# A hybrid Fourier, recurrence and expert layer on one core: A gate tiles between the recurrence heads, adaLN blocks spread, expert buffers at multiples of 512 bytes

## The chip, the cores and the metric

The kernel runs on one core of a Trainium2 chip. The metric is device microseconds of one execution, the median of several runs. The core has a matrix engine (TensorE, PE in the profile; PEld is its weight load), a vector engine (VectorE, DVE), an activation engine (ScalarE, ACT), GpSimd (POOL) and SyncE (SP), which here only issues transfers.

## The reference, cut to what matters

One layer of a diffusion backbone: 512 latent tokens and 256 context tokens of 1024 elements.

```python
z    = modulate(rmsnorm(x, norm1_g), sh1, sc1) @ w_in   # columns: Fourier 512 | X 1024 | G 1024 | A 1024 | B 1024
u    = dwconv(z[X], conv_w, conv_b)                     # width 4, context and latent tokens
r, i = sigmoid(u @ wa + ba), sigmoid(u @ wi + bi)       # 8 heads of 128, two directions
a    = exp(-8 * r * softplus(-lam))
h    = scan over tokens: h = a * h + sqrt(1 - a * a) * i * u    # forward + backward, context first
y    = sigmoid(z[A]) * (fourier(z[F]) @ w_four) + sigmoid(z[B]) * ((gelu(z[G]) * h) @ w_lru)
x    = x + g1 * (y @ w_out)
h2   = modulate(rmsnorm(x, norm2_g), sh2, sc2)
s    = softmax(h2 @ w_router)                           # 16 experts take their 64 best tokens
x    = x + g2 * scatter(s * (silu(xg @ w_gate) * (xg @ w_up)) @ w_down)   # 1024 -> 1536 -> 1024
out  = rmsnorm(x, final_g)
```

`sh1`, `sc1`, `g1` and so on are the six adaLN sections of 1024 columns of `silu(c) @ w_ada + b_ada`.

## The kernel before, in words

Everything before the experts is float32 work on TensorE as three products of split operands: a float32 weight `raw` is split into `wH` (a cast to fp32r, L229) and `wL = raw - wH` (a DVE subtraction, L230), and `mm3` (L426) multiplies H·H, H·L and L·H. Weights come in tiles of 1024 rows × 256 columns (1 MB), listed in `W` (L150 to L173) and loaded by SP in the order of `seq` into three `raw` buffers (`load_next`, L177); `split(j)` consumes tile j, in two halves of 128 × 1024 elements each, and `use(j)` splits the next tile while it hands over this one.

The order of the work is the order of the program: each engine takes its instructions as they are written (`manual_schedule`), and semaphores do the rest. PSUM has two tags of two slots of 2 banks each, `z` (`zt`) and `g` (`gt`); `ct` takes one or the other in turn.

*Recurrence heads.* Eight heads h; for each, 8 k-steps of 6 matmuls (512 latent and 256 context columns, tile `zX` in `z`). In k-steps 4 to 7 of head h, one gate (two matmuls, L674, L675, tile `ga` in `g`, tanh on ACT at L677) of head h−1 follows each step. After the matmuls `conv(h)` (L663, L667) runs on DVE; then `lru(h-1)`: tanh on ACT and `stt` on DVE (L688), exp and sqrt on ACT, `stt` on DVE (L698), a multiplication on GpSimd (L699), twice for two directions, then three scans on DVE (L705, L707, L709) and an addition on GpSimd (L711). At even heads the next X weight is split in the middle of `lru`, its cast on DVE.

*A, G and B tiles.* Eight A tiles follow (24 matmuls of 512 columns, `zcols`), with `a_evac` (tanh on ACT, L750, and a DVE multiplication into `y4`, L751), the last head's gates and `lru`; then eight G tiles (gelu times the recurrence, split into `gH`, `gL`); then eight B tiles, each with a `w_lru` tile; then the output projection `zO` and the routing.

*adaLN.* The first eight blocks of 256 columns are computed before the heads. The other sixteen are done by `ada_acc` (L264: on DVE, eight scaled additions of 128 × 256 elements and a sum, L271 to L276) and `ada_red` (L280: a matmul with ones, L287 or L291, and additions on DVE), one behind each pair of A, G, B or `w_lru` tiles and the last in `zO`.

*Experts.* From 475 us on, 16 experts: gate, up (L1116), `silu`, down (L1210, L1267), scatter (L1132). Their weights, 128 rows × 6144 bytes a load (768 KB), come by SP through a ring of 22 buffers: unit n goes to slot n modulo 22 (`eload`, L834 to L861). Slots 0 to 13 are the pool `ra` on the right side of SBUF, 14 to 18 the pool `rb` and 19 the pool `rc` on the left, 20 and 21 two `held` tiles on the left (`wd`, `we`). A buffer is loaded anew when its user is done.

Of the kernel before, what the change touches and what calls it, by code (L numbers as in the profile page):

```python
# [9 lines left out]
F32 = mybir.dt.float32  # L10
# [7 lines left out]
P = 128  # L18
D = 1024
# [57 lines left out]
def layer(ctx: ExitStack, tc: tile.TileContext, I, out):  # L77
# [48 lines left out]
    eps_t = keep.tile([P, 1], F32, name="eps_t")  # L126
    ones = keep.tile([P, 1], F32, name="ones")
# [4 lines left out]
    cs = keep.tile([P, KD, 32], F32, name="cs")  # L132
# [20 lines left out]
    W += [(cols(w_in, D_F + 256 * i), 8) for i in range(4)]  # L153
    W += [(cols(w_in, D_F + 2 * D + 256 * i), 8) for i in range(4)]
# [5 lines left out]
    J_X, J_A, J_G, J_B, J_O = 2, 6, 10, 14, 22  # L160
# [4 lines left out]
    ada_at = {j: [p] for j, p in zip([J_A] + list(range(J_A + 2, J_O)), range(8, 23))}  # L165
    ada_at[J_O + 1] = [23]
# [97 lines left out]
    def ada_acc(i):  # L264
        for j in ada_at.get(i, ()):
            raw = take("a", j)
            r = [stage.tile([P, 256], F32, tag="acc", bufs=2, name=f"acc{j}_{a}") for a in range(2)]
            m = len(r)
            for k in range(KD):
                if k < m:  # L270
                    dve.tensor_scalar(r[k], raw[:, k, :], cs[:, k, 0:1], None, op0=OP.mult)  # L271
                else:
                    dve.scalar_tensor_tensor(r[k % m], raw[:, k, :], cs[:, k, 0:1], r[k % m], op0=OP.mult, op1=OP.add)
            load_next()
            if m == 2:
                dve.tensor_add(r[1], r[0], r[1])  # L276
            adaq.append((j, r[-1]))
# [32 lines left out]
    zs = st_p.tile([P, NT, 1028], F32, name="zs")  # L310
    rs, ce = zs[:, 0, 0:1024], zs[:, 1, 0:512]
# [368 lines left out]
    def lru(h, mid=None, pre=None):  # L680
        u = U.pop(h)
        r = {(d, i): GP.pop((h, d, i)) for d in range(2) for i in range(2)}
        tps = {}
        for d in range(2):
            q = 8 * d + h
            tps[d] = lr.tile([P, TA], F32, tag="tp", bufs=3, name=f"tp{h}")
            act.activation(tps[d], r[d, 0], AF.Tanh, bias=c2[:, q:q + 1], scale=c2[:, q:q + 1])
            dve.scalar_tensor_tensor(r[d, 1], r[d, 1], 1.0, u, op0=OP.add, op1=OP.mult)  # L688
        if pre:
            pre()  # L690
        for d in range(2):
            q = 8 * d + h
            act.activation(r[d, 0], r[d, 0], AF.Exp, bias=c4n[:, q:q + 1], scale=c4n[:, q:q + 1])
        for d in range(2):
            act.activation(tps[d], tps[d], AF.Sqrt, scale=0.25)
        for d in range(2):
            a, b, s = r[d, 0], r[d, 1], tps[d]
            dve.scalar_tensor_tensor(s, a, 1.0, s, op0=OP.add, op1=OP.mult)  # L698
            pool.tensor_tensor(b, s, b, op=OP.mult)  # L699
        if mid:  # L700
            mid()
        for d in range(2):
            a, b, s = r[d, 0], r[d, 1], tps[d]
            if d == 0:
                dve.tensor_tensor_scan(s, a, b, 0.0, OP.mult, OP.add)  # L705
            else:
                dve.tensor_tensor_scan(s[:, 0:TC][:, ::-1], a[:, 0:TC][:, ::-1], b[:, 0:TC][:, ::-1],  # L707
                                       0.0, OP.mult, OP.add)
                dve.tensor_tensor_scan(s[:, TC:TA][:, ::-1], a[:, TC:TA][:, ::-1], b[:, TC:TA][:, ::-1],  # L709
                                       s[:, 0:1], OP.mult, OP.add)  # L710
        pool.tensor_tensor(yr[:, h, :], tps[0][:, TC:TA], tps[1][:, TC:TA], op=OP.add)  # L711

    GATES = [(0, 0), (0, 1), (1, 0), (1, 1)]
    AT = {4: 0, 5: 1, 6: 2, 7: 3}
    load_gw(0)
    for h in range(H):
        if h % 2 == 0:
            w = SP.pop(J_X + h // 2)
        zf = f2(zt(f"zX{h}"))
        for k in range(KD):  # L720
            wH, wL = ch(w, k, h % 2)
            n = 0
            for a, b, bc in ((wH, hH, cH), (wH, hL, cL), (wL, hH, cH)):
                f, l = k == 0 and n == 0, k == KD - 1 and n == 2
                pe.matmul(zf[:, 512:1024], a, b[:, k, :], start=f, stop=l)
                pe.matmul(zf[:, 256:512], a, bc[:, k, :], start=f, stop=l)
                n += 1
            if h and k in AT:
                gate(h - 1, *GATES[AT[k]])
        if h + 1 < H:  # L730
            load_gw(h + 1)
        conv(h, zf[:, 256:1024])

        def next_split(h=h):
            if h % 2 == 0:
                split(J_X + h // 2 + 1, dve.tensor_copy)
        if h:
            lru(h - 1, next_split)
        else:
            next_split()  # L740


# [10 lines left out]
    def last_gates(k):  # L753
        if k % 2:
            gate(H - 1, *GATES[k // 2])
        if k == 1:
            a_evac(0, zz_[0])
        if k == 4:
            split(J_A + 1)

    for i in range(4):
        w = SP.pop(J_A + i) if i < 2 else use(J_A + i)
        zz_ = []
        for c in range(2):
            z = ct(c if i else 0, "zA")
            zz_.append(z)
            zcols(w, z, c, None if i or c == 0 else last_gates)
        evacs = lambda: [a_evac(2 * i + c, zz_[c]) for c in range(0 if i else 1, 2)]
        if i == 1:
            lru(H - 1, pre=lambda: split(J_A + 2, dve.tensor_copy), mid=evacs)  # L770
            close_lr()
            close_hc()
        else:
            evacs()
        ada_red()
        ada_acc(J_A + i)

    gp, close_gp = sb("gp", "right")
    gH = gp.tile([P, H, T], F32R, name="gH")
    gL = gp.tile([P, H, T], F32R, name="gL")  # L780
    for i in range(4):
        w = use(J_G + i)
        for c in range(2):
            z = ct(c, "zG")
            zcols(w, z, c)
            j = 2 * i + c
            act.activation(z, z, AF.Gelu_apprx_tanh)
            dve.tensor_mul(yr[:, j, :], z, yr[:, j, :])
            act.copy(gH[:, j, :], yr[:, j, :])
            dve.tensor_sub(gL[:, j, :], yr[:, j, :], gH[:, j, :].bitcast(F32))  # L790
        ada_red()
        ada_acc(J_G + i)

# [3 lines left out]
    for i in range(4):  # L797
        w = use(J_B + 2 * i)
        th = sg.tile([P, 2, 512], F32, tag="th", bufs=2, name="thB")
        for c in range(2):  # L800
            z = ct(c, "zB")
            zcols(w, z, c)
            act.activation(th[:, c, :], z, AF.Tanh, scale=0.5)
        ada_red()
# [19 lines left out]
    rings = [None] * 3  # L824
    rings[0], close_ra = sb("ra", "right")
# [124 lines left out]
    ada_red()  # L950
# [354 lines left out]
    close_ra()  # L1305
    close_stage()
# [32 lines left out]
```

## Time and the profile before

| | |
|---|---|
| Runs, median (lowest to highest of 3) | 1206.58 us (1205.19 to 1206.61) |
| The profiled execution: time, span | 1205.73 us, 1203.9 us |
| Mean granted clock of TensorE | 0.984 |
| Busy: PE, PEld, DVE, ACT, POOL | 95%, 57%, 47%, 24%, 9% |
| Moved by DMA, mean | 368.01 MB, 306 GB/s |

The span is the profiled execution from its first to its last instruction; what the device counts around it makes up the rest of its time. Busy shares are means over stages with different limits, so they are read by stage. In the page's strip of 40 slices (30.1 us each) the heads, A and G tiles lie in slices 4 to 11, the experts from slice 16 on. A timeline's row gives start, duration, engine, line, operation, output and inputs, and in brackets the idle time before it and what ended it; "issue" is a wait that no event of the profile explains.

### The profile page before, as it was taken

Reading aid. Unit: us, or ns where it says so; the run is one execution under the profiler, and the core shown is the slowest. Engines: PE = TensorE matmul, PEld = TensorE weight load, DVE = VectorE, ACT = ScalarE, POOL = GpSimd, SP = SyncE. Lnnn points to the kernel's source line nnn. Section 1 sums busy time; section 2 is a strip of 40 time slices with the busy share of each in tenths; the row PEclk is TensorE's granted clock in tenths of the full one; section 3 lists DMA queues with packets and bytes.
Section 4 is the critical chain, followed back from the end, with each engine's and each line's share of the span. In section 5 each row is a group of like instructions: output and inputs, shape, how many; then the busy total and the mean of one; then the engine's idle time right before and its main releaser. Section 6 shows DMA issues by size and latency. Waiting matters only on the chain. (4 is left out here: it accounts for less than half of the span.)

```text
span 1203.9 us, 16716 instructions
## 1 busy us (share of the span) xinstructions
PE 1148.4 (95%) x6891; PEld 684.3 (57%) x6891; DVE 564.3 (47%) x1053; ACT 286.4 (24%) x448; POOL 112.9 (9%) x118
## 2 busy tenths in 40 slices
PE   8979988899999999999999999999999999999986
PEld 5768766588888897545445445445345345345333
DVE  5566899996776675233332332332232232232024
ACT  5443766644322223101001001001001001001004
POOL 5164443310000000000000000000000000000002
PEclk9989988999999999999999999999999999999998
DMA  8922011155555495899899999999999999999995
GB/s 308 300 89 88 18 53 53 35 173 177 188 180 191 149 390 206 313 379 418 356 422 419 418 420 421 418 419 421 420 417 421 421 418 418 422 421 418 419 400 211
DMA packets 115435, 368.01 MB, mean 306 GB/s; under 512 B 8912, under 2 KB 61656, under 8 KB 115232
## 3 DMA queue, kind: packets, MB, share of 16 engines
q1 hardware_dynamic: 112688, 363.52, 76.9%
q0 software_dynamic: 1088, 2.18, 0.6%
q10 hardware_dynamic: 1584, 1.25, 0.4%
q8 instruction: 54, 0.88, 0.3%
q14 instruction: 21, 0.17, 0.0%
HBM read 364.43 MB, written 2.10 MB: 304 GB/s over the span
## 5 line engine op out<-in xcount | busy, mean ns | idle before, releaser
L1116 PE MATMUL U<-ew,g 128*64 128x384 f32 x928 | 167.5, 494 | 8.7 <-DMA ew<-in_w_up_e 8.6
L1116 PE MATMUL G<-ew,g 128*64 128x384 f32 x960 | 171.7, 493 | 3.8 <-DMA ew<-in_w_gate_e 3.5
L1135 DVE TENSOR_TENSOR x<-x,sc 128x512 f32<-128x512 f32 x120 | 77.1, 684 | 104.2 <-PE sc L1132 104.2
L1116 PEld LDWEIGHTS G<-ew,g 128*64 128x64 f32 x960 | 62.8, 136 | 87.0 <-issue 62.6
L1116 PEld LDWEIGHTS U<-ew,g 128*64 128x64 f32 x928 | 60.0, 136 | 90.6 <-issue 56.9
L1247 POOL TENSOR_TENSOR o<-x,ew 128x512 f32<-128x512 f32 (+1 forms) x8 | 7.8, 1003 | 926.7 <-ACT o L1243 926.7
L1213 DVE SCALAR_TENSOR_TENSOR wc<-Y,gc,g 128x512 f32<-128x512 f32 x15 | 11.3, 751 | 148.6 <-PE Y L1210 148.6
L1210 PE MATMUL Y<-ew,wa 128*64 128x512 f32 x312 | 75.7, 598 | 2.2 <-ACT wa L1199 2.2
L1210 PE MATMUL Y<-ew,wd 128*64 128x512 f32 x324 | 77.5, 594 | 0.0
L1199 ACT COPY wa<-T 128x384 f32<-128x384 f32 x16 | 7.7, 479 | 254.2 <-PE T L1198 254.2
L230 DVE TENSOR_TENSOR wL<-raw,wH 128x1024 fp32r<-128x1024 f32 x48 | 62.9, 1341 | 2.0 <-ACT wH L229 1.6
L1172 ACT ACTIVATE wc<-G 128x768 f32<-128x768 f32 x16 | 13.0, 811 | 181.7 <-PE G L1116 181.7
L1210 PEld LDWEIGHTS Y<-ew,wd 128*64 128x64 f32 x324 | 24.2, 137 | 49.1 <-issue 41.7
L1088 PEld LDWEIGHTS xg<-wa,xn 128*128 128x128 f32 x448 | 51.1, 192 | 0.2
L1088 PE MATMUL xg<-wa,xn 128*128 128x128 f32 x448 | 51.2, 275 | 0.0
L1054 DVE TENSOR_SCALAR wc<-wa,score 128x128 bf16<-128x128 f32 (+3 forms) x63 | 24.0, 381 | 56.7 <-ACT wa L1047 56.7
L1210 PEld LDWEIGHTS Y<-ew,wa 128*64 128x64 f32 x312 | 21.8, 136 | 45.0 <-issue 34.6
L1216 ACT CAST wb<-wc 128x512 fp32r<-128x512 f32 x15 | 9.3, 619 | 156.1 <-DVE wc L1213 156.1
L674 PE MATMUL ga<-u,gw 128*128 128x512 f32 x64 | 36.0, 645 | 10.0 <-issue 9.9
L1132 PEld LDWEIGHTS sc<-wb 64*128 64x128 f32 x240 | 23.6, 184 | 35.9 <-issue 35.9
L229 ACT CAST wH<-raw 128x1024 fp32r<-128x1024 f32 x38 | 37.9, 1045 | 17.8 <-PE zO L426 9.9
L699 POOL TENSOR_TENSOR th<-tp,th 128x768 f32<-128x768 f32 x16 | 35.0, 2206 | 49.2 <-DVE tp L698 49.2
(360 smaller groups left out, 2183.9 us busy)
## 6 DMA issues: line engine op xcount, KB each, us to landing
ew<-in_w_gate_e SPq DMA_DIRECT2D x120, 768.0 KB, 14.9
ew<-in_w_up_e SPq DMA_DIRECT2D x116, 768.0 KB, 14.9
ew<-in_w_down_e SPq DMA_DIRECT2D x113, 768.0 KB, 14.9
raw<-in_w_ada SPq DMA_DIRECT2D x24, 1024.0 KB, 5.4
raw<-in_w_in SPq DMA_DIRECT2D x16, 1024.0 KB, 4.9
wd<-in_w_down_e SPq DMA_DIRECT2D x7, 768.0 KB, 12.3
we<-in_w_down_e SPq DMA_DIRECT2D x7, 768.0 KB, 12.9
wd<-in_w_up_e SPq DMA_DIRECT2D x6, 768.0 KB, 14.6
```

Of the source, the lines that this page charges most:

```text
L229: (copy or act.copy)(wH[:, a], raw[:, a])
L230: dve.tensor_sub(wL[:, a], raw[:, a], wH[:, a].bitcast(F32))
L674: pe.matmul(gf[:, 512:1024], gw[:, d, i, :], u[:, TC:TA], start=True, stop=True)
L699: pool.tensor_tensor(b, s, b, op=OP.mult)
L1054: dve.tensor_scalar(GT[c][:, 0:m], sB[:, 0:m], s, None, op0=OP.is_lt)
L1088: pe.matmul(a[k // 4][:, P * (k % 4) + q.start:P * (k % 4) + q.stop], XN[n // 2][:, n % 2, P * k:P * k + P], oh[:, n, q], start=n == 0, st ...
L1116: pe.matmul(t[64 * f:64 * f + 64, n, 0:384], xg[:, k, c:c + CAP], w[:, o:o + 384], start=k == 0, stop=k == KD - 1, tile_position=(0, 64 * f))
L1132: pe.matmul(a[dh][:, c], w, v, start=j == 0, stop=j == 1, tile_position=(64 * dh, 0))
L1135: dve.tensor_add(xs, xs, a[dh])
L1172: act.activation(v3(sl), G[:, :, 0:384], AF.Silu)
L1210: pe.matmul(yp[64 * dh:64 * dh + 64, :], hT[j // 3][:, j % 3, 64 * f:64 * f + 64], w[:, 512 * i:512 * i + 512], start=f == 0 and j == 0, s ...
L1213: dve.scalar_tensor_tensor(y, yp, gc[:, e % 3:e % 3 + 1], g2, op0=OP.mult, op1=OP.mult)
```

## The change

An A tile (24 matmuls, a `g` slot) follows the X matmuls of each head; its evacuation `a_evac` comes at k-step 3 of the next head, ahead of the gates of k-steps 4 to 7. `W` alternates X and A weights. The A weights are split in halves at k-steps 3 and 5 of even heads, the X weights behind the convolution of odd heads; all these casts are on ACT. `lru` is cut: its scans come one head later, ahead of the convolution. Four adaLN blocks move into the odd heads (between sqrt and the L698 `stt`), each with its `ada_red` at k-step 6; three stay in G, two come in the first B tile, one after each later B or `w_lru` tile, none in `zO`. The last head's gates, scans and `lru` go into the first two rounds of G, whose evacuation runs one round late, from one slot of two banks. The router's weights `wr` are loaded at the start of the heads by ACT's queue and stay in `keep`; `cs` moves to an earlier pool, with a contiguous copy `csv` of its first column. The total size of `keep` stays the same. A tile of 480 bytes, `edge`, is allocated on the right ahead of the pool `ra`, so that its buffers begin 480 bytes lower.

```diff
@@ -123,13 +123,14 @@
-    eps_t = keep.tile([P, 1], F32, name="eps_t")
-    ones = keep.tile([P, 1], F32, name="ones")
+    one_eps = keep.tile([P, 2], F32, name="one_eps")
+    eps_t, ones = one_eps[:, 0:1], one_eps[:, 1:2]
-    cs = keep.tile([P, KD, 32], F32, name="cs")
+    csv = keep.tile([P, KD], F32, name="csv")
+    wr = keep.tile([P, KD, 32], F32, name="wr")
@@ -150,20 +151,23 @@
-    W += [(cols(w_in, D_F + 256 * i), 8) for i in range(4)]
-    W += [(cols(w_in, D_F + 2 * D + 256 * i), 8) for i in range(4)]
+    for i in range(4):
+        W.append((cols(w_in, D_F + 256 * i), 8))
+        W.append((cols(w_in, D_F + 2 * D + 256 * i), 8))
-    J_X, J_A, J_G, J_B, J_O = 2, 6, 10, 14, 22
+    J_X, J_G, J_B, J_O = 2, 10, 14, 22
-    ada_at = {j: [p] for j, p in zip([J_A] + list(range(J_A + 2, J_O)), range(8, 23))}
-    ada_at[J_O + 1] = [23]
+    ada_at = {j: [p] for j, p in zip([J_X + 1, J_X + 3, J_X + 5, J_X + 7, J_G + 1, J_G + 2], range(8, 14))}
+    ada_at[J_G + 3] = [14]
+    ada_at[J_B] = [15, 16]
+    ada_at.update({j: [p] for j, p in zip(range(J_B + 1, J_O), range(17, 24))})
@@ -262,15 +266,16 @@
-        for j in ada_at.get(i, ()):
+        for j in ada_at.get(i, ())[:1]:
+            ada_at[i] = ada_at[i][1:]
-                    dve.tensor_scalar(r[k], raw[:, k, :], cs[:, k, 0:1], None, op0=OP.mult)
+                    dve.tensor_scalar(r[k], raw[:, k, :], csv[:, k:k + 1], None, op0=OP.mult)
                 else:
-                    dve.scalar_tensor_tensor(r[k % m], raw[:, k, :], cs[:, k, 0:1], r[k % m], op0=OP.mult, op1=OP.add)
+                    dve.scalar_tensor_tensor(r[k % m], raw[:, k, :], csv[:, k:k + 1], r[k % m], op0=OP.mult, op1=OP.add)
@@ -308,6 +313,7 @@
+    cs = st_p.tile([P, KD, 32], F32, name="cs")
@@ -346,6 +352,7 @@
+    dve.tensor_copy(csv, cs[:, :, 0])
@@ -677,7 +684,9 @@
-    def lru(h, mid=None, pre=None):
+    LR = {}
+
+    def lru(h, mid=None):
@@ -686,19 +695,21 @@
-        if pre:
-            pre()
+        if mid:
+            mid()
-        if mid:
-            mid()
+        LR[h] = r, tps
+
+    def scans(h):
+        r, tps = LR.pop(h)
@@ -710,86 +721,99 @@
+    def zcols(w, o, c, tick=None):
+        for k in range(KD):
+            mm3(o, ch(w, k, c), (hH[:, k, :], hL[:, k, :]), k == 0, k == KD - 1)
+            if tick:
+                tick(k)
+
+    def a_evac(j, z):
+        act.activation(z, z, AF.Tanh, scale=0.5)
+        dve.scalar_tensor_tensor(y4[j][:, :], z, 1.0, y4[j][:, :], op0=OP.add, op1=OP.mult)
+
     GATES = [(0, 0), (0, 1), (1, 0), (1, 1)]
-    AT = {4: 0, 5: 1, 6: 2, 7: 3}
+    zA = {}
+
+    def tail_of(h, k, at):
+        if k == at[0] - 1:
+            a_evac(h, zA.pop(h))
+        if k in at:
+            gate(h, *GATES[at.index(k)])
+
+
     load_gw(0)
+    dve.memset(wr, 0.0)
+    nc.scalar.dma_start(wr[:, :, 0:NE], I["w_router"][0].rearrange("(k p) e -> p k e", p=P))
-            w = SP.pop(J_X + h // 2)
+            wx = SP.pop(J_X + h)
+            if not h:
+                split(J_X + 1)
-            wH, wL = ch(w, k, h % 2)
+            wH, wL = ch(wx, k, h % 2)
-            if h and k in AT:
-                gate(h - 1, *GATES[AT[k]])
+            if h:
+                tail_of(h - 1, k, (4, 5, 6, 7))
+            if h and h % 2 == 0 and k in (3, 5):
+                split_half(J_X + h + 1, k // 5)
+            if k == 6:
+                ada_red()
+        if h > 1:
+            scans(h - 2)
         conv(h, zf[:, 256:1024])
-
-        def next_split(h=h):
-            if h % 2 == 0:
-                split(J_X + h // 2 + 1, dve.tensor_copy)
+        if h % 2:
+            split(J_X + h + 1)
+        if h % 2 == 0:
+            wg = SP.pop(J_X + h + 1)
+        zA[h] = gt("zA")[:, 0, :]
+        zcols(wg, zA[h], h % 2)
         if h:
-            lru(h - 1, next_split)
-        else:
-            next_split()
-
-
-    def zcols(w, o, c, tick=None):
-        for k in range(KD):
-            mm3(o, ch(w, k, c), (hH[:, k, :], hL[:, k, :]), k == 0, k == KD - 1)
-            if tick:
-                tick(k)
-
-    def a_evac(j, z):
-        act.activation(z, z, AF.Tanh, scale=0.5)
-        dve.scalar_tensor_tensor(y4[j][:, :], z, 1.0, y4[j][:, :], op0=OP.add, op1=OP.mult)
-
-    def last_gates(k):
-        if k % 2:
-            gate(H - 1, *GATES[k // 2])
-        if k == 1:
-            a_evac(0, zz_[0])
-        if k == 4:
-            split(J_A + 1)
+            lru(h - 1, lambda: ada_acc(J_X + h) if h % 2 else None)
+
+    zG = {}
+
+    def g_evac(i):
+        z = zG.pop(i)
+        for c in range(2):
+            j = 2 * i + c
+            act.activation(z[:, c, :], z[:, c, :], AF.Gelu_apprx_tanh)
+            dve.tensor_mul(yr[:, j, :], z[:, c, :], yr[:, j, :])
+            act.copy(gH[:, j, :], yr[:, j, :])
+            dve.tensor_sub(gL[:, j, :], yr[:, j, :], gH[:, j, :].bitcast(F32))
+
+    def g_tick(k):
+        tail_of(H - 1, k, (4, 5, 6, 7))
+        if k in (3, 5):
+            split_half(J_G + 1, k // 5)
-        w = SP.pop(J_A + i) if i < 2 else use(J_A + i)
-        zz_ = []
+        w = use(J_G + i) if i else SP.pop(J_G)
+        zG[i] = (gt if i == 2 else zt)("zG")
         for c in range(2):
-            z = ct(c if i else 0, "zA")
-            zz_.append(z)
-            zcols(w, z, c, None if i or c == 0 else last_gates)
-        evacs = lambda: [a_evac(2 * i + c, zz_[c]) for c in range(0 if i else 1, 2)]
+            zcols(w, zG[i][:, c, :], c, None if i or c else g_tick)
+        if i == 0:
+            scans(H - 2)
+            lru(H - 1)
+            continue
         if i == 1:
-            lru(H - 1, pre=lambda: split(J_A + 2, dve.tensor_copy), mid=evacs)
+            scans(H - 1)
-        else:
-            evacs()
-        ada_red()
-        ada_acc(J_A + i)
-
-    gp, close_gp = sb("gp", "right")
-    gH = gp.tile([P, H, T], F32R, name="gH")
-    gL = gp.tile([P, H, T], F32R, name="gL")
-    for i in range(4):
-        w = use(J_G + i)
-        for c in range(2):
-            z = ct(c, "zG")
-            zcols(w, z, c)
-            j = 2 * i + c
-            act.activation(z, z, AF.Gelu_apprx_tanh)
-            dve.tensor_mul(yr[:, j, :], z, yr[:, j, :])
-            act.copy(gH[:, j, :], yr[:, j, :])
-            dve.tensor_sub(gL[:, j, :], yr[:, j, :], gH[:, j, :].bitcast(F32))
+            gp, close_gp = sb("gp", "right")
+            gH = gp.tile([P, H, T], F32R, name="gH")
+            gL = gp.tile([P, H, T], F32R, name="gL")
+        g_evac(i - 1)
+    g_evac(3)
@@ -799,8 +823,10 @@
-            zcols(w, z, c)
+            zcols(w, z, c, None if i else lambda k: k == 6 and ada_red())
             act.activation(th[:, c, :], z, AF.Tanh, scale=0.5)
+            if i == 0 and c == 0:
+                ada_acc(J_B)
@@ -822,6 +848,8 @@
+    edge, close_edge = open_pool("edge", side="right")
+    edge.tile([P, 120], F32, name="edge")
@@ -863,9 +891,6 @@
-    wr = rt.tile([P, KD, 32], F32, name="wr")
-    dve.memset(wr, 0.0)
-    nc.scalar.dma_start(wr[:, :, 0:NE], I["w_router"][0].rearrange("(k p) e -> p k e", p=P))
@@ -941,13 +966,11 @@
-            ada_acc(J_O + 1)
-    ada_red()
@@ -1303,6 +1326,7 @@
+    close_edge()
```

## Rows read from the trace of the kernel before

**Rows 1.** Windows of busy time: stretch and length in us, engines, clock, DMA share, GB/s
```profile
97.00:320.00 223.00, 208.53 (x914) 160.83 (x913) 185.58 (x236) 119.32 (x135) 62.15 (x46) 0.96 0.29 97
...
800.00:1142.00 342.00, 329.55 (x2072) 149.62 (x2068) 95.76 (x211) 27.09 (x52) 0.00 (x0) 1.00 1.02 419
```

**Rows 2.** Waits of PE, 97 to 320 us: total us, times, longest
```profile
PE ga L674 <- issue: 9.9, 3, 4.5
PE zA L426 <- DVE u L667: 4.2, 1, 4.2
```

**Rows 3.** Timeline of PE: start, duration, operation, and idle before with its releaser
```profile
110.83 1.02 PE L674 MATMUL ga<-u,gw 128*128 128x512 f32 x2
...
118.97 0.58 PE L725 MATMUL zX<-hH,wH 128*128 128x512 f32 x1
...
124.45 1.02 PE L674 MATMUL ga<-u,gw 128*128 128x512 f32 x2
...
158.00 2.04 PE L674 MATMUL ga<-u,gw 128*128 128x512 f32 x2 [4.47 <-issue]
...
162.50 1.02 PE L674 MATMUL ga<-u,gw 128*128 128x512 f32 x2
...
273.18 0.59 PE L291 MATMUL adb<-acc,ones 128*128 128x256 f32 x2
...
319.69 0.50 PE L287 MATMUL adb<-ones,acc 128*128 128x1 f32 x4
```

**Rows 4.** Timeline of DVE, from 140 to 168 and from 262 to 274 us
```profile
148.15 0.68 DVE L229 CAST wH<-raw 128x1024 fp32r<-128x1024 f32 x1
148.87 1.23 DVE L230 TENSOR_TENSOR wL<-raw,wH 128x1024 fp32r<-128x1024 f32 x1
150.01 1.75 DVE L705 TENSOR_TENSOR_SCAN tp<-th,th 128x768 f32<-128x768 f32 x1
...
153.58 1.05 DVE L663 TENSOR_SCALAR u<-zX,col 128x768 f32<-128x768 f32 x1
...
157.82 1.82 DVE L688 SCALAR_TENSOR_TENSOR th<-th,u 128x768 f32<-128x768 f32 x2
...
163.62 3.38 DVE L705 TENSOR_TENSOR_SCAN tp<-th,th 128x768 f32<-128x768 f32 x1 [1.71 <-POOL th L699]
...
262.58 1.28 DVE L751 SCALAR_TENSOR_TENSOR y<-zA,y 128x512 f32<-128x512 f32 x2
263.78 0.60 DVE L271 TENSOR_SCALAR acc<-raw,cs 128x256 f32<-128x256 f32 x2
...
267.13 2.35 DVE L230 TENSOR_TENSOR wL<-raw,wH 128x1024 fp32r<-128x1024 f32 x2
```

**Rows 5.** Timeline of GpSimd (POOL), one head's two multiplications
```profile
142.43 4.72 POOL L699 TENSOR_TENSOR th<-tp,th 128x768 f32<-128x768 f32 x2 [4.74 <-DVE tp L698]
```

**Rows 6.** Waits of SP's queue, 475 to 1189 us: total us, times, longest
```profile
SPq L861 <- DMA we<-g: 13.4, 1, 13.4
```

**Rows 7.** Timeline of SP's queue, 590 to 640 us: the expert loads issued
```profile
593.33 3.97 SPq L861 DMA_DIRECT2D ew<-in_w_gate_e  x8
597.40 11.16 SPq L861 DMA_DIRECT2D ew<-in_w_up_e  x6
610.12 0.33 SPq L861 DMA_DIRECT2D wd<-in_w_up_e  x1
612.00 0.33 SPq L861 DMA_DIRECT2D we<-in_w_up_e  x1
```

**Rows 8.** Windows of busy time while the expert ring streams; the last column is GB/s
```profile
614.00:624.00 10.00, 10.00 (x70) 4.43 (x68) 4.08 (x7) 0.62 (x1) 0.00 (x0) 1.00 1.02 426
632.00:650.00 18.00, 17.84 (x148) 12.40 (x146) 6.27 (x18) 1.24 (x3) 0.00 (x0) 1.00 1.02 416
655.00:665.00 10.00, 10.00 (x62) 3.98 (x60) 2.80 (x5) 0.62 (x1) 0.00 (x0) 1.00 1.02 422
673.00:691.00 18.00, 17.84 (x126) 8.12 (x124) 7.39 (x19) 1.93 (x4) 0.00 (x0) 1.00 1.02 415
```

**Rows 9.** DMA issues: count, KB each, us from issue to landing
```profile
we<-in_w_up_e SPq DMA_DIRECT2D x6, 768.0 KB, 14.6
```

**Rows 10.** Timeline of PE where the experts end
```profile
1182.65 0.83 PE L1267 MATMUL Y<-ew,wa 128*64 128x256 f32 x5 [0.36 <-DMA ew<-in_w_down_e]
```

More of the change, by code (lines that the diff above doesn't have):

```diff
@@ L711, in lru @@
         pool.tensor_tensor(yr[:, h, :], tps[0][:, TC:TA], tps[1][:, TC:TA], op=OP.add)
-    GATES = [(0, 0), (0, 1), (1, 0), (1, 1)]
-    AT = {4: 0, 5: 1, 6: 2, 7: 3}
-    load_gw(0)
-    for h in range(H):
-        if h % 2 == 0:
-            w = SP.pop(J_X + h // 2)
-        zf = f2(zt(f"zX{h}"))
-        for k in range(KD):
-            wH, wL = ch(w, k, h % 2)
[L722 to L727, printed above, removed]
-            if h and k in AT:
-                gate(h - 1, *GATES[AT[k]])
-        if h + 1 < H:
-            load_gw(h + 1)
-        conv(h, zf[:, 256:1024])
-        def next_split(h=h):
-            if h % 2 == 0:
-                split(J_X + h // 2 + 1, dve.tensor_copy)
-        if h:
-            lru(h - 1, next_split)
-        else:
-            next_split()
     def zcols(w, o, c, tick=None):
@@ L751, in a_evac @@
         dve.scalar_tensor_tensor(y4[j][:, :], z, 1.0, y4[j][:, :], op0=OP.add, op1=OP.mult)
-    def last_gates(k):
-        if k % 2:
-            gate(H - 1, *GATES[k // 2])
-        if k == 1:
-            a_evac(0, zz_[0])
-        if k == 4:
-            split(J_A + 1)
+    GATES = [(0, 0), (0, 1), (1, 0), (1, 1)]
+    zA = {}
[4 more added lines that the diff above has]
+            gate(h, *GATES[at.index(k)])
+    load_gw(0)
@@ new lines, in layer @@
+    dve.memset(wr, 0.0)
+    nc.scalar.dma_start(wr[:, :, 0:NE], I["w_router"][0].rearrange("(k p) e -> p k e", p=P))
+    for h in range(H):
+        if h % 2 == 0:
+            wx = SP.pop(J_X + h)
+            if not h:
+                split(J_X + 1)
+        zf = f2(zt(f"zX{h}"))
+        for k in range(KD):
+            wH, wL = ch(wx, k, h % 2)
+            n = 0
+            for a, b, bc in ((wH, hH, cH), (wH, hL, cL), (wL, hH, cH)):
+                f, l = k == 0 and n == 0, k == KD - 1 and n == 2
+                pe.matmul(zf[:, 512:1024], a, b[:, k, :], start=f, stop=l)
+                pe.matmul(zf[:, 256:512], a, bc[:, k, :], start=f, stop=l)
+                n += 1
+            if h:
[4 more added lines that the diff above has]
+                ada_red()
+        if h + 1 < H:
+            load_gw(h + 1)
+        if h > 1:
+            scans(h - 2)
+        conv(h, zf[:, 256:1024])
+        if h % 2:
+            split(J_X + h + 1)
+        if h % 2 == 0:
+            wg = SP.pop(J_X + h + 1)
+        zA[h] = gt("zA")[:, 0, :]
+        zcols(wg, zA[h], h % 2)
+        if h:
+            lru(h - 1, lambda: ada_acc(J_X + h) if h % 2 else None)
```

## The prediction

> **What bounds the kernel now.** I read the busy time by stage first. It cuts the run in two. In the first half TensorE (PE) has the work but doesn't always get it: from the first recurrence head to the end of the G tiles, 97 to 320 us, it is busy 208.5 of 223.0 us at a mean clock of 0.96, while VectorE (DVE) is busy 185.6 us and the DMA queues idle for 71% of the time [rows 1]. In the experts, 800 to 1142 us, it is the other way round: the DMA engines are full (share 1.02, 419 GB/s) and PE has 342.0 − 329.6 = 12.4 us to spare [rows 1].
>
> The waits of PE then name what it lacks in the first half: three waits before a recurrence gate, 9.9 us, and one of 4.2 us before the A tiles, for the convolution on DVE [rows 2]. The timeline shows a second price. Before the gate at 158.00 PE stands for 4.47 us, and after it the pair of gate matmuls takes 2.04 us where the same pair takes 1.02 at 162.50: the lower of its two clock levels. From 158.00 to 162.50 are 4.50 us for one gate and one k-step, work of 2.31 (below), so the stall costs 2.2 us more than itself [rows 3].
>
> What does PE need at the full clock? Between the last gate of one head and the first of the next are five k-steps of six matmuls: (124.45 − 118.97)/5 = 1.096 us each. A head with four gates takes 124.45 − 110.83 = 13.62, so a gate takes (13.62 − 8 × 1.096)/4 = 1.21. The eight G tiles with their four adaLN reductions take 319.69 − 273.18 = 46.5, or 5.81 a tile [rows 3]. The stage is one head without gates (8.77), seven with (95.3), the last four gates (4.8) and sixteen tiles (93.0): 202 us. Against 223 there are 21 us to win: 14.1 of waits, the rest mostly low clock.
>
> **The order of A tiles and heads.** Today a pair of heads brings DVE: two convolutions of 157.82 − 153.58 = 4.24, two pairs of L688 at 1.82, two of L698, which has the same form, three scans of 153.58 − 150.01 = 3.57 per head, and one weight split of two casts (0.68) and two subtractions (150.01 − 148.87 = 1.14): 8.5 + 3.6 + 3.6 + 7.1 + 3.6 = 26.5 us [rows 4]. PE needs 27.2 for the pair. But GpSimd's two multiplications take 4.72 [rows 5], and a DVE operation with two SBUF inputs that meets one is nearly doubled: the scan at 163.62 takes 3.38 where that at 150.01 takes 1.75 [rows 4]. Four meetings in a pair at 1.6 us make it 32.9, so DVE sets the pace, and PE stands.
>
> Afterwards a pair of heads carries two A tiles as well, 27.2 + 11.6 = 38.9 us of PE. DVE gets two splits without casts (4 × 1.14 = 4.6), two A evacuations ((263.78 − 262.58)/2 = 0.6 each), one adaLN block (267.13 − 263.78 = 3.35) and its reduction (about 0.9, estimated as two small additions): 8.5 + 3.6 + 3.6 + 7.1 + 4.6 + 1.2 + 3.35 + 0.9 = 32.9 us [rows 4]. With four collisions it is 39.3, with none 32.9; if every multiplication stopped DVE for its whole length, 2 × 4.72 more, 42.3. I take two of the four at 1.6, since the scans move behind the next head, by when the multiplications are over, and an evacuation or a split lies there instead: 36.1, under 38.9. The ten casts that DVE loses (the splits of the X tiles and two of A) go to ScalarE, busy 119 of 223 us [rows 1]; at 0.68 each, even doubled, they are under 14 us there, hidden. The weights' loads come in another order, the same number in the stage but for two adaLN blocks, at a DMA share of 0.29 [rows 1]: hidden too.
>
> *Where it is tight.* The A tile takes one of two `g` slots of PSUM, which the gates take in turn. The second gate of an even head therefore waits until a_evac has emptied the A tile. From the end of the odd head's X matmuls DVE does convolution 4.24, two subtractions 2.28, L688 1.82, the adaLN block 3.35, L698 1.83 and the evacuation 0.6: 14.1 us. In the same time PE does the last gate 1.21, the tile 5.81, five k-steps 5.48, a gate and another step 2.31: 14.8. The margin is 0.7 us, a single collision (1.6) takes it away, and beyond it each microsecond stalls PE by one: the gate and all X matmuls behind it. Behind the evacuation itself stand, on ScalarE, the gates' tanh and the casts, on DVE the next subtractions, all of them due later. From nothing to 1.6 at three places, I take 1.5 in all.
>
> *Where it fails.* The last head's gates ride in the first G tile, whose k-step is 5.81/8 = 0.73 and not 1.096: PE then has 14.8 − 6 × 0.37 = 12.6 us for DVE's 14.1, a wait of 1.5 to 2. In G, DVE has for every two tiles (11.6 us) an adaLN block 3.35, a split 2.3, two evacuations of two operations, and, in the first two rounds, the scans of heads 6 and 7 (3.57 each) and the last head's L688 and L698 (3.6): some 13 to 15 us. A reduction on PE that waits for a block then stands, and the next tile behind it. I put 3.5 us there, between 0 and twice that. Together 5.3, and after the longer of them a piece of low clock, 1 of the possible 2.2.
>
> The sum: 21 − 5.3 − 1 − 1.5 = 13 us; between 8 (twice those stalls) and 21.
>
> **What is moved without a price.** The router's weights come early by ScalarE's queue, into memory that is free; only DVE's memset of 256 columns is added there, under the first head's 8.8 us of PE. Without cover it would cost about the 0.6 of a 256-column pair [rows 4]. The contiguous copy of the adaLN factors is one tiny operation. The last adaLN block leaves the output projection, where DVE isn't needed for long; I take 0, and at best one block is won, 3.35 [rows 4]. The first B tile takes an additional reduction, under 0.3 of PE, that G no longer does.
>
> **What the experts make of 13 us.** Up to 593 us the loads wait for the work: SP stands 13.4 us before it can refill a buffer that holds g [rows 6]. From 593.33 on SP issues without a gap [rows 7], and the end is a matmul that waits for a transfer [rows 10]. So everything ahead moves by the gain, and the stream starts and ends that much earlier: 1:1. PE, with 12.4 us to spare in 342, keeps up.
>
> **The buffers.** The ring has 22 slots. Counted from the allocations, 14 of them (the pool on the right side) begin 32 bytes under a multiple of 512, the eight others at one. Slots 20 and 21 are the `wd` and `we` of SP's issues at 610 and 612.00 [rows 7]; a load lands 14.6 us after its issue [rows 9], so the eight aligned loads land up to about 626.6, and the 14 others after it. Just there the rate changes: 426 GB/s at 614 to 624, 416 at 632 to 650, 422 at 655 to 665, 415 at 673 to 691 [rows 8]. Mean 424 against 415.5 is 2.0%; with all slots aligned the stream needs 14/22 × 2.0% = 1.28% less time, and from 593 to 1182 that is 7.5 us. Above it lies nothing that the rows show; below it 0, if the slots differ by something else than the offset. The new tile of 480 bytes moves the 14 to multiples of 512.
>
> The Trainium skill bears on this in "DMA: Bandwidth & Descriptors", section "How a descriptor splits into AXI transactions": a transaction must start at a 256-byte boundary, so a piece that starts off one pays additional beats. For pieces of 6144 bytes that start 224 past a boundary I work out 199 beats of 32 bytes against 192, 3.6%, as an estimate; the sum by it would be 13 us instead of 7.5. The trace shows 2.0%, and I stay with that.
>
> **Forecast.** 1205.7 − 13 − 7.5 = 1185.2 us for the profiled execution. Its span of 1203.9 has 1.8 around it, which stay; it lies 0.85 under the median of the runs, so 1186 us.
>
> **Rivals.**
> *The offset is worth nothing* (0.16). All 14 slow slots also lie in one pool on one side, and the offset can't be told from the place. Against it: size, source, queue and order of the loads are the same in both sorts [rows 7, 8], and only the place in SBUF differs. Time: 1186 + 7.5 = 1193.5. The Trainium skill speaks for this rival in "SBUF — State Buffer", section "A bandwidth-pool intuition that's wrong (but worth ruling out)", by which HBM and not SBUF is nearly always the end-to-end bound; in this trace loads of equal size from the same HBM differ by where they land [rows 8], which speaks against it.
>
> *DVE stays the bound* (0.15). If all four multiplications meet an operation of two inputs, a pair of heads takes between 39.3 and 42.3; at the middle, 40.8, four pairs lose 4 × 1.9 = 7.6 us, the front wins 5.4 instead of 13, and the time is 1193.5. For it speaks that DVE's 32.9 us alone fill 85% of a pair, against it that the scans move away from the multiplications.
>
> *The slot stalls every head* (0.04), the other side. If a_evac comes late at each head as convolutions do now, each of seven heads pays a stall of 4.5 and 2.2 of low clock: 46.9 − 28.5 (the 21 and 7.5 that the change may win) = 18 us slower, 1225. It decides from a price of 28.5/7 = 4 us a head.
>
> **Chances and range.** The forecast has 0.65: its own range is 1178.5 (the whole 21) to 1191 (8). Both rivals at 1193.5 lie inside 1178.5 to 1195, which leaves the two together (1201) and the slot outside. Faster by over 0.2% (2.4 us, what a measurement can tell from nothing) 0.92, same 0.03, slower 0.05.
>
> **What would show it.** X matmuls of a head begin 19.5 to 20 us after those of the one before; no gate waits 4 us; the clock is 1.00 in the heads; the first B tile begins at 304 to 309; stalls of 2 to 4 us remain in G only; the expert stream shows 424 to 426 GB/s in every stretch. Wrong would be: a wait of over 2 us at the second gate of even heads, DVE over 95% busy in the heads, or 415 GB/s still in 14 of 22 loads.

## The result and the profile after

The change makes the kernel faster: 1190.81 us median (1189.56 to 1194.27, four runs) against 1206.59, a ratio of 0.9872 with a 95% interval of 0.9848 to 0.9896. Forecast were 1186, so 15.8 us came of the 20.6. The profiled execution took 1191.67 us with a span of 1189.9.

The windows of busy time of both kernels, cut at the same four events (first matmul of the first head, of B, of the output projection, of the experts), tell where the time went. Columns as in [rows 1]. Before:

```profile
97.06:320.05 222.99, 208.52 (x914) 160.82 (x913) 185.52 (x236) 119.37 (x135) 62.09 (x46) 0.96 0.29 98
320.05:412.98 92.93, 92.93 (x414) 75.48 (x414) 61.52 (x120) 25.30 (x33) 0.00 (x0) 1.00 0.55 186
412.98:482.30 69.32, 68.03 (x590) 60.91 (x588) 46.08 (x118) 20.02 (x38) 0.00 (x0) 1.00 0.69 267
482.30:1203.90 721.60, 692.67 (x4453) 324.41 (x4452) 216.50 (x480) 71.81 (x147) 7.76 (x8) 0.99 0.99 401
```

After:

```profile
98.42:305.48 207.06, 203.87 (x914) 158.40 (x913) 170.75 (x224) 125.71 (x140) 66.61 (x46) 0.99 0.31 103
305.48:406.62 101.14, 97.06 (x417) 78.17 (x416) 67.89 (x134) 27.01 (x36) 0.00 (x0) 0.97 0.55 186
406.62:475.50 68.88, 67.47 (x588) 60.49 (x588) 42.03 (x107) 19.92 (x38) 0.00 (x0) 1.00 0.63 252
475.50:1189.90 714.40, 688.54 (x4438) 325.09 (x4452) 216.38 (x480) 71.79 (x147) 7.77 (x8) 1.00 0.98 405
```

| stage | before | after | difference | forecast |
|---|---|---|---|---|
| start to the first head | 97.06 | 98.42 | +1.4 | 0 |
| heads, A, G | 222.99 | 207.06 | −15.9 | −13 |
| B | 92.93 | 101.14 | **+8.2** | 0 |
| output projection, routing | 69.32 | 68.88 | −0.4 | 0 |
| experts | 721.60 | 714.40 | −7.2 | −7.5 |

The start isn't the change's doing: of the ten other kernels profiled below, the nine that share its code began their heads at 96.3 to 99.1 us. The profiled executions differ by 14.1 us, the medians by 15.8; the start's 1.4 is most of that gap. What remains is a front that did better than forecast, an expert stage as forecast, and a loss of 8.2 us in a stage to which the prediction gave nothing.

The waits of PE after, up to 320 us, answer to [rows 2]; the waits in 300 to 420 us follow as a second view:

```profile
PE ga L681 <- ACT th L684: 2.0, 1, 2.0
PE adb L292 <- DVE acc L281: 1.5, 2, 1.2
```

```profile
PE adb L292 <- DVE acc L281: 4.1, 2, 3.8
```

Gone are 9.9 us before gates and 4.2 before the A tiles. In all eight heads no wait is left: PE is busy 50.00 of 50.00 us from 150 to 200. The first new wait, 2.0 us, is at the second gate of the last head, in the first G tile. It ends with the first gate's tanh on ScalarE:

```profile
255.50 0.68 DVE L732 SCALAR_TENSOR_TENSOR y<-zA,y 128x512 f32<-128x512 f32 x1
255.52 0.90 ACT L684 ACTIVATE th<-ga,lru_c 128x768 f32<-128x768 f32 x1
256.48 1.13 PE L681 MATMUL ga<-u,gw 128*128 128x512 f32 x2 [2.02 <-ACT th L684]
```

The evacuation on DVE ends at 256.18, the tanh at 256.42, and the gate starts 0.06 us later. ScalarE has been busy 12.14 of the 12.19 us up to there: two casts of the next weights, `lru`'s tanh, exp and sqrt, two table loads of 1.28 us each, the A tile's tanh, another cast and the gate's tanh itself. The long wait is in B, and the timeline of DVE there shows why (start, duration, line, operation):

```profile
306.74 0.69 DVE L790 TENSOR_TENSOR gL<-yr,gH 128x512 fp32r<-128x512 f32 x1 [0.69 <-ACT gH L789]
...
307.42 0.61 DVE L276 TENSOR_SCALAR acc<-raw,csv 128x256 f32<-128x256 f32 x2
...
310.78 0.68 DVE L788 TENSOR_TENSOR yr<-zG,yr 128x512 f32<-128x512 f32 x1
...
314.13 0.69 DVE L790 TENSOR_TENSOR gL<-yr,gH 128x512 fp32r<-128x512 f32 x1 [0.69 <-ACT gH L789]
315.08 2.36 DVE L234 TENSOR_TENSOR wL<-raw,wH 128x1024 fp32r<-128x1024 f32 x2 [0.26 <-ACT wH L233]
...
317.43 0.60 DVE L276 TENSOR_SCALAR acc<-raw,csv 128x256 f32<-128x256 f32 x2
...
320.44 0.42 DVE L281 TENSOR_TENSOR acc<-acc,acc 128x256 f32<-128x256 f32 x1
```

B begins at 305.48, but DVE is still evacuating the third pair of G tiles, then does the block that G left (307.42 to 310.8), the fourth pair (to 314.8), the split for the first `w_lru` tile (to 317.4), and only then the first of B's two blocks, to 320.86. Its reduction stands in PE's order behind the seventh k-step of the second tile of the first B pair. The timeline of PE:

```profile
310.91 0.61 PE L292 MATMUL adb<-one_eps,acc 128*128 128x1 f32 x4 [0.29 <-DVE acc L281]
...
321.01 0.91 PE L292 MATMUL adb<-one_eps,acc 128*128 128x1 f32 x4 [3.79 <-DVE acc L281]
321.79 0.77 PE L433 MATMUL zB<-hH,wH 128*128 128x512 f32 x1
322.36 0.63 PE L433 MATMUL zB<-hL,wH 128*128 128x512 f32 x1
```

PE stands 3.79 us, and then a matmul takes 0.63 where it takes 0.40 at the full clock; the granted clock, the third column from the right, is 0.69 from 318 to 326 us:

```profile
318.00:326.00 8.00, 4.99 (x14) 4.15 (x15) 6.83 (x19) 2.48 (x3) 0.00 (x0) 0.69 0.77 262
```

The two waits in B, 4.1 us, are half of the 8.2. The low clock is most of the rest, some 3 us (an estimate: up to 328 us a matmul follows the one before by 0.43 us, where it is 0.23 at the full clock).

The experts answer to [rows 8]. The windows of the changed kernel show 424 at 632 and at 673 us where before 416 and 415 stood. The two short windows, which were fast before (426 and 422), read 421 and 422, so 10 us are too short to tell 424 from 426. The mean from 800 to 1142 us is 424, where it was 419 [rows 1]:

```profile
614.00:624.00 10.00, 10.00 (x70) 4.55 (x70) 3.44 (x7) 1.40 (x2) 0.00 (x0) 1.00 1.01 421
632.00:650.00 18.00, 17.78 (x121) 11.52 (x120) 4.26 (x9) 2.51 (x6) 0.00 (x0) 1.00 1.02 424
655.00:665.00 10.00, 10.00 (x74) 4.76 (x72) 4.01 (x7) 0.00 (x0) 0.00 (x0) 1.00 1.01 422
673.00:691.00 18.00, 17.78 (x113) 7.24 (x112) 3.24 (x7) 0.88 (x2) 0.00 (x0) 1.00 1.02 424
800.00:1142.00 342.00, 330.95 (x2083) 151.89 (x2088) 97.64 (x209) 27.68 (x53) 0.00 (x0) 1.00 1.02 424
```

### The profile page after: what moved, and what is told of

It reads as the page before. It is cut to its first block, busy times and chain, and to the rows that moved or that the text cites. A ratio compares the mean times of both kernels' runs of the same rounds, so it can differ in the third digit from the quotient of the medians.

```text
span 1189.9 us, 16700 instructions
## 1 busy us (share of the span) xinstructions
PE 1144.1 (96%) x6873; PEld 685.3 (58%) x6891; DVE 552.6 (46%) x1044; ACT 294.1 (25%) x457; POOL 117.1 (10%) x118
## 5 line engine op out<-in xcount | busy, mean ns | idle before, releaser
L233 ACT CAST wH<-raw 128x1024 fp32r<-128x1024 f32 x48 | 48.2, 1044 | 22.7 <-PE zO L433 9.9
L708 POOL TENSOR_TENSOR th<-tp,th 128x768 f32<-128x768 f32 x16 | 38.5, 2427 | 63.1 <-DVE tp L707 63.1
L278 DVE SCALAR_TENSOR_TENSOR acc<-raw,csv,acc 128x256 f32<-128x256 f32 x96 | 39.3, 477 | 0.0
```

Of the source, the lines that this page charges most:

```text
L233: (copy or act.copy)(wH[:, a], raw[:, a])
L278: dve.scalar_tensor_tensor(r[k % m], raw[:, k, :], csv[:, k:k + 1], r[k % m], op0=OP.mult, op1=OP.add)
```

## The experiments

**The offset alone, and the rest alone.** To the kernel before only the 480-byte tile is added; from the changed kernel only that tile is taken.

```diff
+    edge, close_edge = open_pool("edge", side="right")
+    edge.tile([P, 120], F32, name="edge")
     rings[0], close_ra = sb("ra", "right")
```

> The kernel before with the tile of 480 bytes ahead of the pool ra and nothing else of the change. If the 14 buffers were slow for their offset, the stream of loads runs at 423 to 425 GB/s throughout and the time falls by 7 us (7.5 by the prediction, 7.2 by the changed kernel's experts), to about 1199.5. If the offset is worth nothing and the faster stream of the changed kernel came from its other order, 1206.6 and still 415 GB/s in 14 of 22 loads.

> The changed kernel without that tile, so that ra lies 32 bytes under multiples of 512 again. If the offset decides: 7 us slower than the changed kernel, 1197.5 to 1198, with 415 GB/s in 14 of 22 loads, and the stages up to the experts as in the changed kernel: 15 to 16 us won from the first head to the first B tile, 8 lost in the B stage. If it is worth nothing: about 1191.

Measured: with the tile alone 1199.79 us, ratio 0.9941 (0.9923 to 0.9958) to the kernel before, 7.1 us; without it 1197.99, 0.9927 (0.9904 to 0.9949), 7.2 us slower than the changed kernel's median (6.6 by the two ratios to the kernel before). The rate follows the tile in both. Windows of the kernel before with the tile, then of the changed kernel without it:

```profile
632.00:650.00 18.00, 17.78 (x145) 12.32 (x144) 6.27 (x18) 1.25 (x4) 0.00 (x0) 1.00 1.02 424
...
673.00:691.00 18.00, 17.78 (x125) 8.12 (x124) 7.39 (x19) 1.50 (x4) 0.00 (x0) 1.00 1.02 424
```

```profile
632.00:650.00 18.00, 17.78 (x121) 11.52 (x120) 3.95 (x8) 2.51 (x6) 0.00 (x0) 1.00 1.02 418
...
673.00:691.00 18.00, 17.78 (x113) 7.24 (x110) 3.50 (x7) 0.88 (x2) 0.00 (x0) 1.00 1.01 415
```

In the profiled execution with the tile alone the experts take 716.8 us, 4.8 less than before and not 7.2: from 60 to 30 us before its end the stream runs at 384 to 388 GB/s, where the changed kernel's runs at 415 to 418. Two of the profiled executions below, both with the tile, show the same (717.1 and 717.0 us); why stays open.

By the medians the two halves of the change add up: the offset gives 7, the order of the front the rest. The pool stays on its side and in its place but for 480 bytes, so place and side are ruled out as the cause.

**Which offset.** The tile is cut to 224 bytes (buffers at 256 past a multiple of 512) and to 448 (at 32 past one).

```diff
-    edge.tile([P, 120], F32, name="edge")
+    edge.tile([P, 56], F32, name="edge")     # offset_256
+    edge.tile([P, 112], F32, name="edge")    # offset_32
```

> The changed kernel with the tile ahead of ra cut to 224 bytes: the 14 buffers begin at 256 past a multiple of 512. If a boundary of 256 is enough, all loads stream at 423 to 425 GB/s and the time is the changed kernel's, 1191. If it must be 512, 415 GB/s in 14 of 22 loads and about 1198.

> The changed kernel with the tile at 448 bytes: the buffers begin 32 bytes past a multiple of 512 instead of 32 short of one. If every start off a boundary costs the same, 415 GB/s in 14 of 22 loads and 1198. If the cost is that of the bytes fetched ahead of the start (an estimate by the rule of the Trainium skill, "DMA: Bandwidth & Descriptors", section "How a descriptor splits into AXI transactions": 193 beats for 192 here, 199 for 192 at 480), the rate falls by 0.5% at most, to about 422, and the time is 1191 to 1193.

Measured: 1189.29 us (0.9858, 0.9839 to 0.9877) at 256 and 1196.22 (0.9916, 0.9897 to 0.9935) at 32. Windows at 256 and at 32:

```profile
632.00:650.00 18.00, 17.84 (x117) 11.28 (x118) 3.00 (x8) 2.50 (x6) 0.00 (x0) 1.00 1.02 424
673.00:691.00 18.00, 17.78 (x111) 7.30 (x110) 4.20 (x9) 1.50 (x3) 0.00 (x0) 1.00 1.02 426
```

```profile
632.00:650.00 18.00, 17.83 (x120) 11.34 (x119) 3.19 (x8) 2.50 (x6) 0.00 (x0) 1.00 1.02 418
673.00:691.00 18.00, 17.78 (x111) 7.24 (x110) 4.02 (x8) 1.50 (x3) 0.00 (x0) 1.00 1.02 420
```

A boundary of 256 is enough; 512, which the change names, isn't needed. At 32 the experts take 721.7 us and at 256 714.7, a loss of 7.0; at 480 (the kernel without the tile) they take 721.4, a loss of 7.0 to the changed kernel's 714.4. So 32 costs as much as 480, though the rate in the shown stretches falls a little less. The Trainium skill ("DMA: Bandwidth & Descriptors", section "How a descriptor splits into AXI transactions") is right that a start off a 256-byte boundary costs; that the cost grows with the bytes ahead of the start (0.5% at 32, 3.6% at 480 as an estimate from it) these runs don't show. The same holds for "SBUF — State Buffer", section "A bandwidth-pool intuition that's wrong (but worth ruling out)": that HBM and not SBUF is nearly always the end-to-end bound isn't borne out here, since the rate of the stream changes by 1 to 2% with the start address in SBUF alone (415 to 420 GB/s against 424).

**The two blocks in B.** First, one block there and the last one back in the output projection; second, one block behind the first head's A tile, so that the first B pair has one and the projection none.

```diff
-    ada_at[J_B] = [15, 16]
-    ada_at.update({j: [p] for j, p in zip(range(J_B + 1, J_O), range(17, 24))})
+    ada_at.update({j: [p] for j, p in zip(range(J_B, J_O), range(15, 23))})      # one_block_at_b
+    ada_at[J_O + 1] = [23]
...
-            zcols(w, z, c, None if i else lambda k: k == 6 and ada_red())
+            zcols(w, z, c)
...
-            if i == 0 and c == 0:
-                ada_acc(J_B)
```

```diff
+    ada_at = {j: [p] for j, p in zip([J_X, J_X + 1, J_X + 3, J_X + 5, J_X + 7, J_G + 1, J_G + 2, J_G + 3], range(8, 16))}
+    ada_at.update({j: [p] for j, p in zip(range(J_B, J_O), range(16, 24))})      # block_in_first_head
...
             lru(h - 1, lambda: ada_acc(J_X + h) if h % 2 else None)
+        else:
+            ada_acc(J_X)
```

> The changed kernel with one adaLN block instead of two at the first B tile (each later one moves by a tile, the last goes back into the output projection, as before the change). My theory: the stall of 3.8 us in the first B pair and the low clock behind it come from the second block, for which DVE has no room there; then the B stage takes 93 to 94 us instead of 101 and the time is 1183 to 1184. Rival: DVE comes late to B anyhow, because the G evacuation runs a round late and G's splits meet the multiplications on GpSimd; then a stall of 3 us or more stays ahead of the first w_lru tile and less than 3 us are won (1188 or more).

> The changed kernel with one adaLN block behind the first head's A tile, where no lru runs and DVE has room; the blocks in G and B move up by one, so that the first B tile has one and the output projection none. Same theory, 1183 to 1184, if the first heads hold a fifth block without a stall (PE lost nothing in any head of the changed kernel). If the fifth block makes a head wait, a stall shows before a gate in the second head and 2 to 4 us of the gain are missing; if the rival of the run before is right, 1188 or more.

Measured: 1182.33 us (0.9805, 0.9784 to 0.9826) and 1181.73 (0.9791, 0.9771 to 0.981). Windows of the first of the two, cut at the same events as above:

```profile
96.50:303.60 207.10, 203.90 (x914) 158.40 (x912) 170.82 (x224) 125.72 (x140) 66.72 (x46) 0.99 0.32 103
303.60:396.60 93.00, 93.00 (x415) 75.55 (x414) 64.05 (x124) 27.02 (x36) 0.00 (x0) 1.00 0.58 191
396.60:465.90 69.30, 67.90 (x588) 60.87 (x588) 45.84 (x117) 19.92 (x38) 0.00 (x0) 1.00 0.67 265
465.90:1180.60 714.70, 688.60 (x4438) 325.26 (x4452) 216.50 (x480) 71.79 (x147) 7.78 (x8) 1.00 0.99 405
```

B takes 93.00 us instead of 101.14, without any wait and at clock 1.00; heads and experts stay as they were. So the second block, with the early reduction that it forces, is the whole loss: to make room for it (a block takes both `acc` buffers) the first one's reduction stood in the second tile of the pair, and with one block it stands behind the first pair of `w_lru` tiles, where DVE has long caught up. The two come together, and these runs don't separate them. The late G evacuation, with which DVE comes to B, then costs nothing. The second version is the fastest kernel of this study; its heads hold the additional block without a wait (PE is busy 151.00 of 151.00 us from 96 to 247).

**The tight place.** In the fastest version the X weights are cast on DVE again.

```diff
-            split(J_X + h + 1)
+            split(J_X + h + 1, dve.tensor_copy)
```

> The kernel with a block in the first head, and the casts of the X weights (two of 0.68 us in each odd head) on DVE again instead of ScalarE. By the chain from the X matmuls to the evacuation of the A tile, which ended 0.4 us ahead of its gate, DVE is now 1 us late at each of three even heads and the last: waits of about 1 us before the second gate there, 3 of 1 us and one of 3 us instead of 2; with some low clock 4 to 8 us slower, 1186 to 1190. If the slot isn't the tight place, the sum on DVE (36 of 39 us for two heads) still has room and the time stays 1181 to 1183.

Measured: 1187.47 us (0.9849, 0.9825 to 0.9873), 5.7 slower than without. Waits of PE, 97 to 415 us:

```profile
PE adb L290 <- DVE acc L279: 3.5, 1, 3.5
PE ga L679 <- ACT th L682: 0.6, 2, 0.3
PE ga L679 <- DVE y L730: 0.5, 3, 0.2
```

The size was as expected, the places were not. In the even heads the second gate doesn't wait for the evacuation at all. One of them in this run:

```profile
176.93 0.90 ACT L682 ACTIVATE th<-ga,lru_c 128x768 f32<-128x768 f32 x1 [0.50 <-PE ga L680]
177.89 1.13 PE L679 MATMUL ga<-u,gw 128*128 128x512 f32 x2
178.63 0.68 DVE L730 SCALAR_TENSOR_TENSOR y<-zA,y 128x512 f32<-128x512 f32 x1
```

The gate starts 0.74 us ahead of the evacuation and 0.06 behind the end of the first gate's tanh, so its slot is that gate's and not the A tile's. The three waits for the evacuation, 0.2 us each, are in odd heads. At the last head's second gate the wait fell from 2.0 to 0.3 us, although the evacuation there starts 2.5 us behind the gate: the two casts that left ScalarE had caused most of it.

What got slower is the rest of DVE's work. From the first head to G it is 153.0 us instead of 150.8, 2.2 longer. The longest wait came at a reduction in G (293.90 us), which waits for a block, and G grew by 3.2. That DVE's lateness in the heads is carried on to there is argued and not shown.

**The order of the scans.** In the fastest version each head's scans stand again behind its own multiplications.

```diff
-        if h > 1:
-            scans(h - 2)
...
             lru(h - 1, lambda: ada_acc(J_X + h) if h % 2 else None)
+            scans(h - 1)
```

> The kernel with a block in the first head, and each head's scans right behind its own multiplications again, as before the change (ahead of the next A evacuation on DVE), instead of a head later. The A evacuation then stands behind a wait for the first multiplication (2.4 us), a scan that meets the second (3.35) and 1.9 of scans, some 7.5 us more: in even heads 7 us too late for the second gate, in odd heads 2 to 4 us, seven stalls with some low clock behind most: 20 to 40 us slower, 1202 to 1222. This is the rival of the prediction in which the slot stalls every head. If the order of the scans doesn't matter because DVE's sum stays at 36 of 39 us for two heads, under 5 us slower.

Measured: 1218.8 us (1.0096, 1.0064 to 1.0129), 37 slower than without and slower than the kernel before. Waits of PE, 97 to 430 us, and one of them in the timeline:

```profile
PE ga L679 <- DVE y L730: 24.6, 7, 4.1
PE ga L679 <- ACT th L682: 2.0, 1, 2.0
```

```profile
168.39 2.08 PE L679 MATMUL ga<-u,gw 128*128 128x512 f32 x2 [3.01 <-DVE y L730]
170.26 1.06 PE L680 MATMUL ga<-u,gw 128*128 128x256 f32 x2
```

Seven waits for the evacuation of the A tile, 3.5 us each, six of them in the heads and one in the first G tile. Behind some of them a gate's matmul pair takes 2.08 instead of 1.02: the clock is 0.92 in the heads, which take 187 us. This is the prediction's rival of the other side, with its seven stalls and the low clock behind them. The scans' later place is what keeps the change from it.

**The wait in the first G tile.** Twice it was tried to take the 2.0 us before the last head's second gate away, both from the fastest version: the last head's block into the third head, and the last head's block out of the heads, with the last one in the projection.

```diff
-    ada_at = {... zip([J_X, J_X + 1, J_X + 3, J_X + 5, J_X + 7, J_G + 1, J_G + 2, J_G + 3], range(8, 16))}
+    ada_at = {... zip([J_X, J_X + 1, J_X + 2, J_X + 3, J_X + 5, J_G + 1, J_G + 2, J_G + 3], range(8, 16))}   # block_off_last_head
+    ada_at = {... zip([J_X, J_X + 1, J_X + 3, J_X + 5, J_G + 1, J_G + 2, J_G + 3], range(8, 15))}            # no_block_in_last_head
```

> The kernel with a block in the first head, and the block of the last head moved to the third (h = 2), which has no weight split in its chain. The last head's evacuation is then free 3.35 us earlier, and the wait of 2.0 us before the second gate in the first G tile goes; with the low clock behind it 2 to 4 us are won, 1178 to 1180. Rival: DVE is behind in the third and fourth heads and a gate waits there instead, or the G stage takes the 2 us back at its reductions, which wait for DVE; then 1181 to 1183.

> The kernel with a block in the first head, without the block of the last head; the later blocks move back by one, the last into the output projection (0.5 us there, by the run with one block at B). The wait of 2.0 us in the first G tile goes and nothing else in the heads changes: 2 to 3 us faster, 1178.5 to 1180. Rival: G takes it back, since DVE is behind there anyway; then 1181 to 1183 with longer waits at G's reductions.

Measured: 1184.6 us (0.9822, 0.9803 to 0.9841) and 1183.51 (0.9815, 0.9801 to 0.983); neither beats 1181.73, and the intervals overlap with that kernel's. Waits of PE in the first, up to 415 us, and in the second, up to 430, and the evacuation ahead of the gate in the second:

```profile
PE ga L679 <- DVE y L730: 1.9, 3, 1.0
PE zX L756 <- DVE wL L232: 1.2, 1, 1.2
PE adb L290 <- DVE acc L279: 1.0, 1, 1.0
```

```profile
PE adb L291 <- DVE acc L280: 1.0, 1, 1.0
PE ga L680 <- DVE y L731: 1.0, 1, 1.0
```

```profile
255.15 0.69 DVE L731 SCALAR_TENSOR_TENSOR y<-zA,y 128x512 f32<-128x512 f32 x1 [0.80 <-ACT zA L730]
```

In both, 1.0 of the 2.0 us is left at that gate. It now waits for the evacuation, but DVE itself stands idle 0.80 us before it, for the A tile's tanh on ScalarE: without its block DVE is early, and ScalarE's queue is as long as before. In the first run the heads wait 2.1 us as well, where blocks in each of the first four heads are too many: the rival. In the second, heads and G win 1.1 us (204.3 against 205.4), of which the projection takes 0.4 back. My expectation of 2 to 3 us was too high; what is left is under the scatter of the runs.

## Why the prediction held, and where it didn't

*What PE needs* (202 us for the stage) held: 207.06 were measured, of which 3.2 are waits and some 1.7 low clock (0.89 from 290 to 305 us).

*DVE in the heads* held closely: it is busy 35.23 of the 39.06 us of one pair of heads (144.66 to 183.72), put at 36.1 of 38.9. Two collisions in a pair were assumed, and two are there: the subtraction at 178.00 takes 2.26 where its neighbour takes 1.23, and a scan at 197.36 takes 3.35 where another takes 1.75.

*The tight place* was wrong in its mechanism. The second gate of an even head was to wait until DVE has emptied the A tile, 14.1 us against PE's 14.8, and the gates' tanh and the casts on ScalarE were "all of them due later". The run with the casts on DVE shows that this gate takes the first gate's slot and waits for that gate's tanh. In the changed kernel the evacuation ends at 178.08 and that tanh at 178.40; the gate starts at 178.45, 2.45 after the first, where in odd heads it is 2.34. So 0.1 us was paid in each of three even heads; the 1.5 in the sum were not. ScalarE's queue had been compared with the whole stage (119 of 223 us busy) and called hidden; it wasn't summed from the casts to the tanh.

*The wait at the last head's second gate* was put at 1.5 to 2 us for DVE and is 2.0, for ScalarE: the number is right by luck. Two casts fewer on ScalarE take 1.7 of it away, a block fewer on DVE 1.0. *G's reductions* were put at 3.5 and cost 1.2 (the 1.5 above less 0.3 at 310.91, which is in B). Behind them came 1.7 of low clock, where 1 was put. Together with the unused 1.5 that makes the front 2.9 us better than forecast.

*The step that cost most* is the sentence that the first B tile "takes an additional reduction, under 0.3 of PE, that G no longer does". It priced the matmul on PE and not the block on DVE for which the matmul waits. DVE's load had been summed for the heads and for G, and was not carried over the border into B, where G's last block, its last evacuation, a split and B's first block keep DVE from 307.42 to 320.86, and PE asks for the result at 317.2. It cost 8.2 us, half of it waits, most of the rest low clock; taking the second block and the early reduction away gives all of it back.

*The 1:1 step and the ring* held: the experts' stage doesn't change with the front (721.4 us without the tile and 721.60 before; 714.2 to 714.7 with it, but for the three profiled executions of 716.8 to 717.1), and its own 7.2 stand for the forecast 7.5. The rival that the offset is worth nothing has fallen. The rival that DVE is the bound was wrong for the heads, but right in kind for the border of G and B. The rival of the other side was not what this change did, yet it is real: the run with the scans in their old order shows it. Of the signs, two failed: the longest stall is in B and not in G, and two short windows of the stream read 421 and 422 GB/s and not 424 to 426.

In the terms of the sum, B's 8.2 and the ring's 0.3 stand against the forecast, the front's 2.9 and the projection's 0.4 for it: 5.2 us, and the median lies 4.8 above 1186. That it still lies inside the forecast's own range, 1178.5 to 1191, is owed in part to the front's gain, which offset a loss that had no term.

## What to carry to other kernels

When work is spread into the gaps of one engine, sum that engine's queue over the whole stretch in which it stays behind, across the borders of stages, and do it for every engine on the way to the awaited result, not only for the busiest: here ScalarE, busy 126 of 207 us and never the busiest, held a gate. Price an instruction that consumes a result by when the result is there, not by its own length. And look at the start addresses of buffers into which a saturated stream writes: here a tile of 224 bytes is worth 0.6%.

## What was not expected of the hardware

Both starts off a multiple of 256 bytes in SBUF that were tried cost the same (7.0 us of the experts at 480, 7.0 at 32), and 256 is as good as 512.

The low clock behind a wait of PE doesn't grow with the wait. By estimates from the spacing of the matmuls, 1.7 us were lost behind a wait of 1.17 (291.61 us in the changed kernel), nothing behind 2.02 (256.48; the clock is 1.00 from 248 to 270), 1.7 behind 3.55 (293.90 with the casts on DVE), 3.1 behind 3.79 (321.01), and 2.2 behind 4.47 in the kernel before [rows 3].
